# Sixteen experts in another order, a ring of 16 weight slots, and two projections 512 columns wide

## The chip, the cores and the metric

The kernel runs on one core of one Trainium2 chip. The time is device microseconds (us) from the start of the program to its end; the median of three runs is given, and one further execution was profiled. Five engines work from queues of their own: TensorE (PE; its weight loads are listed as PEld), VectorE (DVE), ScalarE (ACT), GpSimd (POOL) and SyncE (SP), which here does nothing but issue transfers from memory (DMA).

## The reference, cut to what matters

One transformer layer over 512 tokens of width 1024, all in float32: a mixer of three branches (forgetting attention, a pooling branch, a state-space branch called SSD), then a mixture of 16 experts.

```
proj = h @ w_in                       # q, k, v, z, xbc, gates, ... are columns of it
y_ssm = ssd_mixer(z, xbc, ...)        # y * silu(z) inside, then @ w_ssm_o
y_att = attention(q, k, v, log_f) @ w_attn_o
merged = g0 * y_att + g1 * y_pool + g2 * y_ssm
x = layer_norm(ALPHA * x + g_m * (merged @ w_out))
# each token goes to 2 of 16 experts, D = 1024, DFF = 512
expert(x, e) = (silu(x @ w1[e]) * (x @ w3[e])) @ w2[e]
x = layer_norm(ALPHA * x + g_f * (sum over its 2 experts of gate * expert(h, e)))
```

## The kernel before

**Stages.** In the profiled execution the normalisation and the modulation take the first 72 us, the state-space branch 72 to 505, pooling 505 to 614, attention 614 to 835, the output projection, the second normalisation and the routing up to about 990, the experts 990 to 1310, and the last sum and normalisation the rest.

**Three products for one.** `mm3` makes a float32 product out of three reduced-precision ones (hi by hi, hi by lo, lo by hi; lines 109 to 111). For that, every weight unit of 1 MB (128 partitions by 2048 numbers) is split in two halves: ACT casts it to the high part (line 90) and DVE, now and then POOL, subtracts that from it (line 91). `proj_n` makes a block of 128 tokens by 256 columns in one PSUM tile of which half is used: 24 matmuls of 256 columns. It serves the z projection (two units for each of four SSD groups) and the value projection (four units), 12 units by 4 blocks by 24 = 1152 matmuls in all.

**Experts in rounds.** `ROUNDS` is a list of 12 rounds. An entry is a position, not a fixed expert: `route` ranks the 12 dynamic experts by their number of tokens, and `RANK` gives the positions, the last one (15) to the largest. A round with one position is a full expert: up to 128 token rows, 6 weight units (four for gate and up, called A here, two for down, called D), 72 matmuls by `mm3`. A round with two is a pair of small experts with up to 64 rows each: 12 units, plain float32 in two column halves of the array (`pair_mm`, line 1364), no splitting. The largest expert gets two blocks of 128 rows; it stands behind the loop, in the end of `experts` and in `last`, and each of its six units is multiplied by both blocks. The loop runs A of round i, the transposes of the rows of round i+1, D of round i-1, the transposes of the activations. A round's result is scattered by token into `y_d` in memory (`put`, an indirect transfer from POOL). The two blocks of the largest expert aren't scattered: they stay on chip (`keep_y`), and matmuls with a one-hot matrix spread them over the tokens (`select`, `spread`, line 1435).

**Weights.** `self.src` is the order in which the 96 units are loaded, written out by hand: A of a round, then D of the round before. `take` hands out the next unit and issues the load of the one 16 places on, into a ring of 17 slots (`SLOTS`); the lower half of a split unit is written into the slot of the unit before it. All these loads stand in SP's queue (line 1201) and run in order; with `OUT = 2` a load is issued when the one two places before it has landed.

**The end.** `begin` (line 1405) loads `y_d` back, 1 MB for each of four token blocks, behind all weights in SP's queue. `gated` weighs the two results of a token and adds the residual: for blocks 0 and 2 two DVE instructions (lines 1419, 1420), for blocks 1 and 3 two scalings on ACT and two additions on POOL (lines 1416, 1417). `add` (line 1428) adds the spread part, and `end` normalises and stores.

Of the kernel before, what the change touches and what calls it, by code (L numbers as in the profile page):

```python
# [8 lines left out]
F32 = mybir.dt.float32  # L9
F32R = mybir.dt.float32r  # L10
# [31 lines left out]
         ("w", 0), ("w", 2), ("w", 4), ("w", 5), ("g", 0), ("x", 5), ("g", 2)]  # L42
Y = ("w", 2), ("w", 4), ("w", 5), ("g", 2)
# [3 lines left out]
ROUNDS = [(0,), (1,), (2,), (3,), (4, 5), (6,), (7,), (8, 9), (10,), (11, 12), (13,), (14,)]  # L47
NR = len(ROUNDS)
FULL = [e for r in ROUNDS if len(r) == 1 for e in r if e >= ST]
RANK = {E - 1: 0, **{e: i + 1 for i, e in enumerate(FULL)},  # L50
        **{e: i + 1 + len(FULL) for i, e in enumerate(e for r in ROUNDS if len(r) == 2 for e in r)}}
# [10 lines left out]
class Net:  # L62
# [375 lines left out]
    def ssd_proj(self, g):  # L438
# [29 lines left out]
        for u in range(2):  # L468
            wt = self.weights(self.I["wu"][5 * g + 3 + u])
            for b in range(NB):  # L470
                ps = self.proj_n(wt, b)
                t = T.tile([P, 256], F32, name="zt", tag="ztan", bufs=2)
                nc.scalar.activation(t, ps[:, :256], AF.Tanh, scale=0.5)
                nc.vector.scalar_tensor_tensor(zs[:, b, u * 256:(u + 1) * 256], t, 1.0, ps[:, :256],
                                               op0=OP.add, op1=OP.mult)
# [101 lines left out]
    def gate(self, br, u, bufs=2, tag="gt", pool=None):  # L577
        wt = self.weights(self.I["wu"][36 + br * 4 + u])
        out = []
        for j in range(2):  # L580
            ps = self.proj_t(wt, j)
            t = (pool or self.T).tile([P, S], F32, name="gt", tag=tag, bufs=bufs)
            self.nc.scalar.activation(t, ps, AF.Tanh, scale=0.5)
            out.append(t)
        return out

    def ssd_branch(self):
# [8 lines left out]
        for u in range(4):  # L596
            gts += self.gate(2, u, bufs=8, tag="gt2")
# [9 lines left out]
    def pool_branch(self):  # L607
# [8 lines left out]
        for g in range(4):  # L616
# [25 lines left out]
            gt = self.gate(1, g)  # L642
# [13 lines left out]
    def att_branch(self):  # L656
# [12 lines left out]
        with self.pool("attg") as self.T:  # L669
# [6 lines left out]
            for u in range(1, 4):  # L676
                gts += self.gate(0, u, bufs=6)
# [18 lines left out]
    def att_heads(self, out, O, gts):  # L696
# [4 lines left out]
        def values(u):  # L701
            wt = self.weights(self.I["wu"][20 + u])
            for b in range(NB):
                ps = self.proj_n(wt, b)
                nc.scalar.copy(vn[:, b, u * 256:(u + 1) * 256], ps[:, :256])

        for u in range(3):
            values(u)
            if not u:
                self.ada_end()  # L710
# [15 lines left out]
        values(3)  # L726
# [194 lines left out]
    def finish(self, X):  # L921
# [28 lines left out]
        down = lambda r: [(e, u) for u in (4, 5) for e in r]  # L950
        for i, r in enumerate(ROUNDS):
            src += [(e, u) for u in range(4) for e in r]
            if i:
                src += down(ROUNDS[i - 1])
        self.src = src + [(E - 1, 0)] + down(ROUNDS[-1]) + [(E - 1, u) for u in range(1, 6)]
        two = {e for r in ROUNDS if len(r) == 2 for e in r}
# [110 lines left out]
    def experts(self, X):  # L1067
# [11 lines left out]
        self.ix = self.K.tile([P, NR + 2, 2], I32, name="ix")  # L1079
# [6 lines left out]
        x = self.stage_x(X, self.xt[0])  # L1086
# [8 lines left out]
        pair = lambda i: i < NR and len(ROUNDS[i]) == 2  # L1095
        for i in range(NR):
            self.slots(X, i + 2)
            self.gather(i + 2)
            n = (self.pair_a if pair(i) else self.stage_a)(X, x, self.take)
            x = (self.pair_x if pair(i + 1) else self.stage_x)(X, self.xt[(i + 1) % 2])  # L1100
            if i:
                (self.pair_d if pair(i - 1) else self.stage_d)(X, a, self.ix[:, i - 1, 1:2], self.take)
            a = self.pair_t(X, *n) if pair(i) else self.stage_t(X, *n)
            if i == 4:
                self.weigh()
                more()
            if i == 4:
# [3 lines left out]
        keep = self.F2.tile([P, 2048], F32R, name="keep", tag="fraw0", bufs=1)  # L1111
        xs = [x, self.stage_x(X, self.xt[(NR + 1) % 2], self.spare())]
        pg = [self.mm_tile() for _ in range(2)]
        for u in range(2):
            w = self.take()
            for c in range(2):
                self.unit_a(pg[c], xs[c], w, u)
            if not u:
                self.stage_d(X, a, self.ix[:, NR - 1, 1:2], self.take)
                self.select(keep[:, D:])  # L1120
# [6 lines left out]
        return xs, pg, w, wd, keep  # L1127

    def last(self, X, xs, pg, w, wd, keep):
        nc, v = self.nc, self.nc.vector  # L1130
        pu = [self.mm_tile() for _ in range(2)]
        for c, u in ((0, 0), (1, 0), (0, 1)):
            self.unit_a(pu[c], xs[c], w[u], u)
        a = self.glu(pg[0], pu[0])
        self.unit_a(pu[1], xs[1], w[1], 1, (0, 1))
        t = [self.turn(X, a)]
        self.unit_a(pu[1], xs[1], w[1], 1, (2, 3))
        self.yx = [X.tile([P, 2, D], F32R, name="yx", tag="xraw5", bufs=1), self.F2.tile([P, 2, D], F32R, name="yx", tag="fraw1", bufs=1)]
        h = [slice(0, 512), slice(512, D)]

        def down(c, i):
            ps = self.mm_tile()
            ah, al = t[c]
            hi, lo = wd[i]
            for k in range(4):
                kc = slice(k * 512, (k + 1) * 512)
                self.mm3(ps, ah[:, k], al[:, k], hi[:, kc], lo[:, kc], k == 0, k == 3)
            return ps
# [4 lines left out]

        y = self.F.tile([P, D], F32, name="yb", tag="yb", bufs=1)
        ps = down(0, 0)
        a = self.glu(pg[1], pu[1])
        self.gated(0, 2)
        t.append(self.turn(X, a, keep))
        keep_y(0, 0, ps)
        self.gated(2, 4)  # L1160
        ps = down(0, 1)
        keep_y(0, 1, ps)
        ps = down(1, 0)
        keep_y(1, 0, ps)
# [12 lines left out]
    def select(self, room):  # L1177
        nc = self.nc
        self.sel = room[:, :].rearrange("p (c t) -> p c t", c=2)
        self.wy = self.K.tile([P, 2], F32, name="wy")  # L1180
        pw = self.aux_tile()
        for c, pos in enumerate((self.pp[:, :, ND - 1], self.pe)):
            g = self.K.tile([P, NB, P], F32, name="sel", tag="fr", bufs=1)
            pt = self.aux_tile()
            self.match(g, pos)
            for b in range(NB):
                self.transpose(pt[:, b * P:(b + 1) * P], g[:, b])
            for b in range(NB):
                nc.tensor.matmul(pw[:, c:c + 1], g[:, b], self.we1[:, b:b + 1], start=b == 0, stop=b == NB - 1)
# [16 lines left out]
    def take(self):  # L1206
# [9 lines left out]
        with ExitStack() as st:  # L1216
            if i in (1, 2, 3):
                st.enter_context(self.tc.issue_after(self.seen.ins))
                pool = (0, 1) if i == 3 else ()
# [3 lines left out]
            w = self.halves(raw, room, self.slot(i - (4 if self.whole[i - 1] else 1), F32R), pool)  # L1223
# [16 lines left out]
    def slots(self, X, r):  # L1240
# [3 lines left out]
        es = ROUNDS[r] if r < NR else (E - 1,)  # L1244
        pos = [self.pe if r > NR else self.p1[:, :, e] if e < ST else self.pp[:, :, e - ST] for e in es]
# [48 lines left out]
    def stage_a(self, X, x, take):  # L1294
        pg = []
        for m in range(2):
# [3 lines left out]
            pg.append(ps)  # L1300
        return pg

    def stage_t(self, X, g, u, room=None):
        return self.turn(X, self.glu(g, u), room)

    def glu(self, g, u):
        nc = self.nc
        a = self.K.tile([P, 512], F32, name="a", tag="fr", bufs=1)
        self.silu = nc.scalar.activation(a, g, AF.Silu)
        self.prod = nc.vector.tensor_tensor(a, a, u, OP.mult)  # L1310
        return a
# [55 lines left out]
    def pair_a(self, X, x, take):  # L1367
        pg = []
        for m in range(2):
# [3 lines left out]
            pg.append(ps)  # L1373
        return pg

    def pair_t(self, X, g, u):
        a = self.glu(g, u)
        pt = self.aux_tile()
# [21 lines left out]
    def begin(self, X):  # L1400
        nc = self.nc
        self.ys, self.zs = [], []
        for b in range(NB):
            y = self.slot(SLOTS.index(Y[b]))[:, :].rearrange("p (k d) -> p k d", k=2)
# [205 lines left out]
    def overflow(self, X):  # L1610
# [20 lines left out]
        rank, star = (K.tile([P, ND], F32, name=nm) for nm in ("rank", "star"))  # L1631
# [7 lines left out]
        v.tensor_copy(star, oh[:, ND - 1])  # L1639
# [12 lines left out]
        v.tensor_scalar(pe, pp[:, :, ND - 1], 128.0, None, op0=OP.subtract)  # L1652

        def more():
            n[0] = 0
            rooms[0] = K.tile([P, 512], F32, name="room", tag="fr", bufs=1)
            w1 = self.we1 = K.tile([P, NB], F32, name="we1")
            t, g1 = T(NB, ND), T(NB)
            for k in range(2):
# [155 lines left out]
```

## Time and profile before

| | us |
|---|---|
| median of three runs | 1335.49 (1333.13 to 1340.77) |
| profiled execution, its own time | 1343.89 |
| its span | 1341.9 |
| TensorE busy in the span | 1257.7 (94%) |
| VectorE, ScalarE, GpSimd busy | 920.7, 597.7, 241.4 |
| moved by DMA | 224.81 MB |

The profiled execution is 8.4 us, or 0.6%, above the median. In the views, `L109` is line 109 of the kernel; `mm<-whi,ht` names the destination and the operands by their names in the program; a row of waits reads "who waits <- for whom: total us, times, longest". The granted clock of TensorE is 1.00 at 2.4 GHz and 0.50 at 1.2 GHz; a stretch between them had both. Matmuls overlap: a start-to-start distance is the cost of one in a row of them, not its listed length.

### The profile page before, as it was taken

The page shows a single profiled execution, that of the slowest core. Times are in us where ns is not written, and L with a number is a line of the kernel's source. Part 1 is how long each engine was busy: PE and PEld are TensorE (multiplying, and loading weights), DVE is VectorE, ACT ScalarE, POOL GpSimd, SP SyncE. Part 2 cuts the span into 40 slices and gives each one's busy share as a digit, 9 for nine tenths or more (in the row PEclk, how much of TensorE's full clock was granted, in tenths as well). Part 3 has the DMA queues.
Part 4 walks back from the last instruction along what each step waited for, and adds up shares of the span by engine and source line. Part 5 has one row for each costly group of instructions (what it writes and reads, how often), then busy time and mean ns, then how long its engine had stood idle before and what let it go on. Part 6 is the DMA issues. An engine that isn't in the chain of part 4 may idle for free. (4 is left out here: it accounts for less than half of the span.)

```text
span 1341.9 us, 17467 instructions
## 1 busy us (share of the span) xinstructions
PE 1257.7 (94%) x6561; PEld 992.2 (74%) x6561; DVE 920.7 (69%) x1498; ACT 597.7 (45%) x1084; POOL 241.4 (18%) x186
## 2 busy tenths in 40 slices
PE   6999999999999999999999999999859999888992
PEld 3788887887887888889977777888647756535781
DVE  6796856667667348794288888486878786515776
ACT  2456463462462324333357667331236554414642
POOL 3501010010010000000111210132233423203253
PEclk6799999999999999999999999999878998999996
DMA  8421111211211228755211103228567989999941
GB/s 337 157 95 64 63 64 63 95 63 63 95 64 63 94 95 320 262 201 193 94 60 63 63 32 124 96 94 331 204 224 284 332 307 334 345 339 336 328 192 64
DMA packets 37766, 224.81 MB, mean 168 GB/s; under 512 B 5411, under 2 KB 5955, under 8 KB 13488
## 3 DMA queue, kind: packets, MB, share of 16 engines
q1 hardware_dynamic: 31008, 208.54, 43.1%
q0 software_dynamic: 4032, 8.84, 1.8%
q10 hardware_dynamic: 2640, 6.29, 1.3%
q8 instruction: 53, 0.87, 0.3%
q14 instruction: 33, 0.27, 0.1%
HBM read 214.80 MB, written 14.70 MB: 171 GB/s over the span
## 5 line engine op out<-in xcount | busy, mean ns | idle before, releaser
L91 DVE TENSOR_TENSOR raw<-raw,whi 128x1024 fp32r<-128x1024 f32 x234 | 291.9, 1264 | 153.4 <-ACT whi L90 133.0
L90 ACT CAST whi<-raw 128x1024 fp32r<-128x1024 f32 x248 | 252.5, 1053 | 149.5 <-PE mm L110 105.6
L109 PE MATMUL mm<-ht,whi 128*128 128x512 f32 x576 | 232.2, 403 | 0.0
L110 PE MATMUL mm<-ht,whi 128*128 128x512 f32 x576 | 228.8, 397 | 0.0
L111 PE MATMUL mm<-ht,raw 128*128 128x512 f32 x576 | 228.5, 397 | 0.0
L109 PE MATMUL mm<-whi,ht 128*128 128x256 f32 (+1 forms) x448 | 135.9, 304 | 0.6 <-DVE cacc L434 0.4
L111 PE MATMUL mm<-whi,ht 128*128 128x256 f32 (+1 forms) x448 | 135.5, 303 | 0.0
L110 PE MATMUL mm<-raw,ht 128*128 128x256 f32 (+1 forms) x448 | 135.4, 302 | 0.0
L111 PEld LDWEIGHTS mm<-ht,raw 128*128 128x128 f32 x576 | 109.3, 190 | 22.2 <-issue 0.2
L109 PEld LDWEIGHTS mm<-ht,whi 128*128 128x128 f32 x576 | 109.7, 191 | 21.0 <-issue 0.9
L110 PEld LDWEIGHTS mm<-ht,whi 128*128 128x128 f32 x576 | 109.5, 190 | 21.0 <-issue 0.7
L109 PEld LDWEIGHTS mm<-whi,ht 128*128 128x128 f32 x448 | 86.1, 192 | 5.8 <-issue 2.7
L111 PEld LDWEIGHTS mm<-whi,ht 128*128 128x128 f32 x448 | 86.3, 193 | 5.0 <-issue 2.4
L110 PEld LDWEIGHTS mm<-raw,ht 128*128 128x128 f32 x448 | 86.2, 193 | 4.5 <-issue 1.8
L110 PE MATMUL mm<-raw,xh 128*128 128x512 f32 x160 | 67.6, 422 | 11.7 <-DVE raw L91 8.0
L109 PE MATMUL mm<-whi,xh 128*128 128x512 f32 x160 | 66.7, 417 | 2.8 <-ACT whi L90 1.7
L111 PE MATMUL mm<-whi,xl 128*128 128x512 f32 x160 | 65.1, 409 | 0.0
L521 POOL TENSOR_TENSOR y<-xsn,small 128x512 f32<-128x512 f32 x16 | 19.8, 1246 | 227.1 <-ACT xsn L452 139.0
L434 DVE SCALAR_TENSOR_TENSOR cacc<-mm,small,cacc 128x511 f32<-128x511 f32 (+2 forms) x72 | 52.9, 743 | 9.3 <-ACT cacc L432 8.7
L110 PE MATMUL mm<-yl,whi 128*128 128x512 f32 x128 | 53.0, 414 | 0.0
L109 PE MATMUL mm<-yh,whi 128*128 128x512 f32 x128 | 52.1, 407 | 0.0
L111 PE MATMUL mm<-yh,raw 128*128 128x512 f32 x128 | 50.8, 397 | 0.0
(427 smaller groups left out, 2422.9 us busy)
## 6 DMA issues: line engine op xcount, KB each, us to landing
raw<-in_we_dram SPq DMA_DIRECT2D x96, 1024.0 KB, 6.7
raw<-in_wu_dram SPq DMA_DIRECT2D x48, 1024.0 KB, 5.0
ra<-in_wada_dram SPq DMA_DIRECT2D x24, 1024.0 KB, 6.9
raw<-in_wso_dram SPq DMA_DIRECT2D x8, 1024.0 KB, 5.1
x<-in_x_dram SPq DMA_DIRECT2D x8, 512.0 KB, 8.2
y_d<-zero ACTq DMA_DIRECT2D x1, 4096.0 KB, 18.1
raw<-in_wao_dram SPq DMA_DIRECT2D x4, 1024.0 KB, 4.9
raw<-in_wout_dram SPq DMA_DIRECT2D x4, 1024.0 KB, 4.8
```

The costliest lines, as they stand in the source:

```text
L90: h = self.nc.scalar.copy(hi, src)
L91: self.cut = [h, (eng or self.nc.vector).tensor_tensor(lo, src, hi.bitcast(F32), OP.subtract)]
L109: mm(ps, lh, rh, start=first, stop=False)
L110: mm(ps, lh, rl, start=False, stop=False)
L111: self.last_mm = mm(ps, ll, rh, start=False, stop=last)
L434: nc.vector.scalar_tensor_tensor(acc[:, i:], ps[:, :S - i], w(3 - i), acc[:, i:], op0=OP.mult, op1=OP.add)
L521: nc.gpsimd.tensor_tensor(h8(y[:, :]), h8(xsn[:, b]), b8(s[:, S_DSK + g * 8:S_DSK + g * 8 + 8]), OP.mult)
```

## The change

**Rounds.** There are 13: positions 0, 1, 2, 3, the pair (4, 5), 6, the pair (7, 8), the two-block expert (9, 9), then 10, 11, 12, 13, and the pair (14, 15) last. The work is the same: nine full experts, three pairs, one expert with two blocks, 96 units. The two-block expert is a round of the loop (`star_a`, `star_d`), its two results are scattered like the others, and it uses all four PSUM tiles of the name `mm` at a time. Now the last two rounds, expert 13 and the pair, stay on chip and are spread.

**Ring.** 16 slots rather than 17; the room set free is the second block's in the two-block round, later that of a `y_d` block.

**`y_d`.** Three of its four blocks are loaded ahead of the last four weight units in SP's queue, the fourth behind them. The first block needs the last scatter, now that of round 10; the second and third go into slots that the pair's first units leave.

**Projections.** `proj_n` makes 512 columns at once: two units of half the depth, four PSUM tiles open through both, 576 matmuls of 512 columns. The tanh of z and the copy of v take 512 columns too.

**Smaller edits.** The silu of an expert stands directly behind its gate product. Unit 3 is split by DVE alone, no longer by POOL. `more` works out weights for three experts rather than one, about ten small DVE instructions more. `gate` of the branches is renamed.

```diff
 SLOTS = [("f", 0), ("f", 1), ("w", 3), ("w", 1), ("g", 1), ("x", 4), ("x", 0), ("x", 1), ("x", 2), ("x", 3),
-         ("w", 0), ("w", 2), ("w", 4), ("w", 5), ("g", 0), ("x", 5), ("g", 2)]
-Y = ("w", 2), ("w", 4), ("w", 5), ("g", 2)
+         ("w", 0), ("w", 2), ("w", 4), ("w", 5), ("g", 0), ("g", 2)]
-ROUNDS = [(0,), (1,), (2,), (3,), (4, 5), (6,), (7,), (8, 9), (10,), (11, 12), (13,), (14,)]
+ROUNDS = [(0,), (1,), (2,), (3,), (4, 5), (6,), (7, 8), (9, 9), (10,), (11,), (12,), (13,), (14, 15)]
...
-    def proj_n(self, wt, b):
-        hi, lo = wt
-        ps = self.mm_tile()
-        for k in range(KD):
-            c = slice(k * 256, (k + 1) * 256)
-            t = slice(b * P, (b + 1) * P)
-            h, l = self.hs(k)
-            self.mm3(ps[:, :256], h[:, t], l[:, t], hi[:, c], lo[:, c], k == 0, k == KD - 1)
-        return ps
+    def proj_n(self, u, then):
+        ps = [self.mm_tile() for _ in range(NB)]
+        for i in range(2):
+            hi, lo = self.weights(self.I["wu"][u + i])
+            for b in range(NB):
+                t = slice(b * P, (b + 1) * P)
+                for j in range(4):
+                    c = slice(j * 512, (j + 1) * 512)
+                    h, l = self.hs(i * 4 + j)
+                    self.mm3(ps[b], h[:, t], l[:, t], hi[:, c], lo[:, c], i == j == 0, i == 1 and j == 3)
+                if i:
+                    then(b, ps[b])
...
-        self.src = src + [(E - 1, 0)] + down(ROUNDS[-1]) + [(E - 1, u) for u in range(1, 6)]
+        self.src = src + of(NR - 1, (0,)) + of(NR - 2, (4, 5)) + of(NR - 1, range(1, 6))
...
+        self.select(X)
+        pg = self.mm_tile()
+        self.pair_mm(pg, x, 0, [self.take(), self.take()], True, False)
         w = [self.take() for _ in range(2)]
-        wd = [self.take() for _ in range(2)]
-        self.begin(X)
-        self.rows = self.F.tile([P, 2048], F32, name="rows", tag="graw0", bufs=1)
+        raws = [self.take() for _ in range(6)]
+        self.begin(X, range(3))
+        raws += [self.take() for _ in range(4)]
+        self.begin(X, (3,))
...
-                pool = (0, 1) if i == 3 else ()
+                pool = ()
...
+    def star_a(self, X, xs, take):
+        ps = [[self.mm_tile() for _ in range(2)] for _ in range(2)]
+        for m in range(2):
+            for u in range(2):
+                w = take()
+                for c in range(2):
+                    self.unit_a(ps[c][m], xs[c], w, u)
+        out = []
+        for c in range(2):
+            out.append(self.gate_up(self.gate(ps[c][0], X.tile([P, 512], F32, name="a2", tag="al2", bufs=1) if c else None), ps[c][1]))
+        return out
...
+        for i in range(2):
+            ps = self.mm_tile()
+            for k in range(4):
+                kc = slice(k * 512, (k + 1) * 512)
+                self.mm3(ps, act[0][:, k], act[1][:, k], w[i][0][:, kc], w[i][1][:, kc], k == 0, k == 3)
+            keep_y(0, i, ps)
+        self.pair_mm(pg, x, 4, raws[0:2], False, True)
+        a = self.gate(pg)
+        pu = self.mm_tile()
+        self.pair_mm(pu, x, 0, raws[2:4], True, False)
+        self.pair_mm(pu, x, 4, raws[4:6], False, True)
+        a = self.gate_up(a, pu)
         pz = self.sums()
         self.spread(pz, 0, 0)
-        ps = down(1, 1)
+        at = self.pair_t(X, a, self.mm_tile())
+        ps = self.mm_tile()
+        self.pair_mm(ps, at, 0, raws[6:8], True, True)
+        self.gated(0, 2)
+        keep_y(1, 0, ps)
+        self.gated(2, 3)
+        ps = self.mm_tile()
+        self.pair_mm(ps, at, 0, raws[8:10], True, True)
         self.spread(pz, 1, 0)
         keep_y(1, 1, ps)
+        self.gated(3, 4)
```

**Where instructions stand now.** First TensorE in the first SSD group, at the end of the z projection (`ht` are the transposed activations, `whi` and `raw` the high and low parts of a weight unit; the rows on `xdt`, `st` and `xde` are the SSD chunks that stand between). Before:

```order
L109 MATMUL mm<-whi,ht_88 128x256
L110 MATMUL mm<-raw,ht_88 128x256
L111 MATMUL mm<-whi,ht_88 128x256
L519 MATMUL aux<-xdt,sc 128x64 x2
L524 MATMUL aux<-st,cmt 128x512
L529 MATMUL aux<-xde,bmn 128x512
L109 MATMUL mm<-ht_85,whi 128x512
L110 MATMUL mm<-ht_85,whi 128x512
L111 MATMUL mm<-ht_85,raw 128x512
```

And with the change:

```order
L112 MATMUL mm<-whi,ht_88 128x512
L113 MATMUL mm<-raw,ht_88 128x512
L114 MATMUL mm<-whi,ht_88 128x512
L524 MATMUL aux<-xdt,sc 128x64 x8
L534 MATMUL aux<-xde,bmn 128x512
L524 MATMUL aux<-xdt,sc 128x64 x8
L112 MATMUL mm<-ht_85,whi 128x512
L113 MATMUL mm<-ht_85,whi 128x512
L529 MATMUL aux<-st,cmt 128x512
L534 MATMUL aux<-xde,bmn 128x512
```

Each matmul of the projection writes 512 columns rather than 256 and there are half as many; the next product (`mm<-ht_85,whi`) follows in both.

Second, SyncE's queue at the end of the experts (each load of a unit, `raw<-in_we_dram`, has a register instruction ISA ahead of it that picks the expert). Before:

```order
L1201 DMA raw<-in_we_dram 128x2048
L1201 ISA
L1201 DMA raw<-in_we_dram 128x2048
L1028 TENSOR_LOAD nob
L1028 ISA x2
L1405 DMA raw<-y_d 128x2048 x4
L1126 DMA rows<-in_rows_dram 128x1024 x2
```

And with the change:

```order
L1217 DMA raw<-in_we_dram 128x2048
L1457 DMA raw<-y_d 128x2048 x3
L1217 ISA
L1217 DMA raw<-in_we_dram 128x2048
L1217 ISA
L1217 DMA raw<-in_we_dram 128x2048
L1217 ISA
L1217 DMA raw<-in_we_dram 128x2048
L1217 ISA
L1217 DMA raw<-in_we_dram 128x2048
L1457 DMA raw<-y_d 128x2048
L1146 DMA raw<-in_rows_dram 128x1024 x2
```

Three of the four loads of `y_d` have moved ahead of the last four weight units, and all that stands behind them waits for them to be issued.

Third, TensorE at its end (`whi,keep` and `yx,keep` belong to the two-block expert before; `raw,xh` and `raw,ah` are the pair's products after, L1487 the spreading). Before:

```order
L109 MATMUL mm<-whi,keep 128x512
L110 MATMUL mm<-raw,keep 128x512
L111 MATMUL mm<-whi,keep 128x512
L1435 MATMUL aux<-yx,keep 128x512 x8
L1435 MATMUL mm<-yx,keep 128x512 x16
```

And with the change:

```order
L113 MATMUL mm<-raw,ah_10207 128x512
L114 MATMUL mm<-whi,al_10208 128x512
L1415 MATMUL mm<-raw,xh 64x512 x24
L1487 MATMUL aux<-raw 128x512 x8
L156 MATMUL mm<-consts,a 128x128 x4
L1415 MATMUL mm<-raw,ah_10392 64x512 x16
L1487 MATMUL aux<-raw 128x512 x8
L1487 MATMUL mm<-raw 128x512 x16
```

The three-product matmuls of the largest expert are gone from the end; what stands there is the pair's gate and up products (24), its down products (16 in two calls) and the same number of spreading matmuls (32).

## Rows read from the trace of the kernel before

**Rows 1.** The page: span, TensorE's share, granted clock in 40 slices.
```profile
span 1341.9 us, 17467 instructions
...
PE 1257.7 (94%) x6561; PEld 992.2 (74%) x6561; DVE 920.7 (69%) x1498; ACT 597.7 (45%) x1084; POOL 241.4 (18%) x186
...
PEclk6799999999999999999999999999878998999996
```

**Rows 2.** Windows by stage: length; busy PE, PEld, DVE, ACT, POOL; clock; DMA share; GB/s.
```profile
72.00:505.00 433.00, 428.71 (x2380) 357.52 (x2379) 283.41 (x413) 194.16 (x391) 29.57 (x27) 1.00 0.22 74
...
1277.50:1310.00 32.50, 32.07 (x149) 25.87 (x147) 24.76 (x20) 14.54 (x18) 16.18 (x7) 1.00 0.42 171
1310.00:1342.00 32.00, 7.62 (x24) 5.59 (x24) 21.41 (x40) 8.32 (x13) 8.86 (x8) 0.66 0.17 67
```

**Rows 3.** Windows as in rows 2, inside the expert stage, by rounds.
```profile
1015.00:1067.00 52.00, 51.92 (x271) 42.14 (x269) 47.17 (x44) 37.67 (x47) 21.24 (x13) 1.00 0.90 323
1067.00:1125.00 58.00, 53.24 (x263) 32.49 (x260) 42.79 (x93) 28.42 (x36) 18.52 (x11) 0.94 0.89 319
1125.00:1186.00 61.00, 57.22 (x280) 32.50 (x280) 28.97 (x32) 22.63 (x29) 15.78 (x10) 1.00 0.94 343
1186.00:1242.00 56.00, 48.07 (x215) 23.91 (x211) 22.45 (x26) 18.65 (x25) 12.17 (x8) 0.97 0.94 333
1242.00:1277.00 35.00, 33.13 (x142) 25.64 (x143) 26.21 (x27) 24.74 (x31) 10.44 (x7) 0.95 0.92 334
```

**Rows 4.** Timeline of TensorE in a z projection: start, length, operation.
```profile
273.77 0.28 PE L109 MATMUL mm<-whi,ht 128*128 128x256 f32 x1
...
279.76 0.28 PE L111 MATMUL mm<-whi,ht 128*128 128x256 f32 x1
```

**Rows 5.** Timeline of TensorE in the output projection, 512 columns.
```profile
917.15 0.39 PE L109 MATMUL mm<-whi,ht 128*128 128x512 f32 x1
...
922.19 0.40 PE L110 MATMUL mm<-raw,ht 128*128 128x512 f32 x1
```

**Rows 6.** Waits of SyncE's queue, 1040 to 1300: total, times, longest.
```profile
SPq L1201 <- DMA raw<-in_we_dram: 187.9, 65, 5.5
SPq L1405 <- DMA y_d<-yb,ix: 10.7, 1, 10.7
...
SPq L1201 <- PE mm L111: 0.4, 1, 0.4
```

**Rows 7.** Timeline of SyncE's queue, 990 to 1300.
```profile
997.41 275.70 SPq L1201 DMA_DIRECT2D raw<-in_we_dram  x80
1284.47 1.97 SPq L1405 DMA_DIRECT2D raw<-y_d  x4
```

**Rows 8.** Busy time in 4 us stretches around the last loads.
```profile
1278.00:1282.00 4.00, 4.00 (x24) 3.45 (x23) 3.98 (x4) 2.88 (x5) 3.37 (x3) 1.00 0.00 0
...
1290.00:1294.00 4.00, 4.00 (x18) 3.00 (x16) 2.94 (x3) 1.98 (x2) 0.00 (x0) 1.00 1.01 428
```

**Rows 9.** Gate and up products of one pair (line 1364 alone).
```profile
1067.00:1081.00 14.00, 13.95 (x64) 4.51 (x64) 1.00 0.92 329
```

**Rows 10.** Timeline of TensorE at the end.
```profile
1309.18 0.39 PE L111 MATMUL mm<-whi,keep 128*128 128x512 f32 x1
...
1313.67 3.36 PE L1435 MATMUL aux<-yx,keep 128*128 128x512 f32 x7 [0.23 <-DVE yx L91]
1316.82 3.97 PE L1435 MATMUL mm<-yx,keep 128*128 128x512 f32 x16
```

**Rows 11.** Timeline of VectorE at the end.
```profile
1319.45 0.69 DVE L1428 SCALAR_TENSOR_TENSOR z<-mm,z 128x512 f32<-128x512 f32 x1 [1.36 <-PE mm L1435]
```

**Rows 12.** Groups of instructions from 1305 to the end: busy, mean ns.
```profile
L1417 POOL TENSOR_TENSOR z<-raw,z 128x1024 f32<-128x1024 f32 x1 | 3.2, 3223 | 0.1
...
L1416 ACT ACTIVATE raw<-raw,gw 128x1024 f32<-128x1024 f32 x1 | 1.1, 1137 | 0.0
```

**Rows 13.** Timeline of VectorE early in the expert stage.
```profile
1000.28 1.23 DVE L91 TENSOR_TENSOR raw<-raw,whi 128x1024 fp32r<-128x1024 f32 x1 [4.67 <-POOL raw L91]
```

More of the change, by code (lines that the diff above doesn't have):

```diff
@@ L467, in ssd_proj, with gated @@
         zs = T.tile([P, NB, 512], F32, name="zs", tag="zs", bufs=1)
[L468 to L475, printed above, removed]
+        def gated(b, ps):
+            t = T.tile([P, 512], F32, name="zt", tag="ztan", bufs=1)
+            nc.scalar.activation(t, ps, AF.Tanh, scale=0.5)
+            nc.vector.scalar_tensor_tensor(zs[:, b], t, 1.0, ps, op0=OP.add, op1=OP.mult)
+        self.proj_n(5 * g + 3, gated)
         return xsn, sc, cmt, bmn, zs
@@ L701, in values @@
         def values(u):
[L702 to L710, printed above, removed]
+            self.proj_n(20 + 2 * u, lambda b, ps: nc.scalar.copy(vn[:, b, u * 512:(u + 1) * 512], ps))
+        values(0)
+        self.ada_end()
         half = [slice(0, 64), slice(64, P)]
@@ L1094, in experts @@
         a = None
[L1095 to L1100, printed above, removed]
-            if i:
-                (self.pair_d if pair(i - 1) else self.stage_d)(X, a, self.ix[:, i - 1, 1:2], self.take)
-            a = self.pair_t(X, *n) if pair(i) else self.stage_t(X, *n)
+        for i in range(NR - 1):
+            for j in lines[i]:
+                if j + 2 < len(LINES):
+                    self.slots(X, j + 2)
+                    self.gather(j + 2)
+            k = KIND[i]
+            n = self.star_a(X, x, self.take) if k == "S" else (self.pair_a(X, x, self.take) if k == "P" else
+                                                               self.stage_a(X, x[0], self.take))
+            x = rows(i + 1)
+            if i:
+                down(i - 1, a)
+            if k == "S":
+                a = [self.turn(X, n[1], self.room[:, D:])]
+                a.insert(0, self.turn(X, n[0]))
+            else:
+                n = self.gate_up(*n)
+                a = self.pair_t(X, n) if k == "P" else self.turn(X, n)
             if i == 4:
@@ L1110, in experts @@
                         nc.scalar.mul(x1[:, b], x1[:, b], ALPHA)
[L1111 to L1120, printed above, removed]
@@ L1125, in experts, with last @@
+        self.rows = self.slot(6)
         for i in range(2):
             nc.sync.dma_start(self.rows[:, i * D:(i + 1) * D], self.I["rows"][2 + i:3 + i, :].to_broadcast([P, D]))
-        return xs, pg, w, wd, keep
-    def last(self, X, xs, pg, w, wd, keep):
+        return x, a, pg, w, raws
+    def last(self, X, x, act, pg, w, raws):
         nc, v = self.nc, self.nc.vector
[L1131 to L1138, printed above, removed]
-        h = [slice(0, 512), slice(512, D)]
[L1141 to L1148, printed above, removed]
+        self.yx = [self.slot(k, F32R)[:, :].rearrange("p (k d) -> p k d", k=2) for k in (5, 4)]
+        h = [slice(0, 512), slice(512, D)]
+        y = self.F.tile([P, D], F32, name="yb", tag="yb", bufs=1)
@@ L1222, in take @@
                     st.enter_context(self.tc.issue_after(m.ins))
[L1223 removed]
+            w = self.halves(raw, room, self.slot(i - (4 if i and self.whole[i - 1] else 1), F32R), pool)
         self.halved = self.cut
@@ L1773, in _layout @@
         us.append(unit((x0 + 2048 + i * P, P), (x0 + 2560 + i * P, P)))
-        us += [unit((z0 + i * 512 + j * 256, 256)) for j in range(2)]
-    us += [unit((v0 + i * 256, 256)) for i in range(4)]
+        us += wide(z0 + i * 512)
+    us += wide(v0) + wide(v0 + 512)
     us += [unit((q0 + i * P, P), (k0 + i * P, P)) for i in range(8)]
```

165 lines of the change are left out of this document (100 added, 65 removed).

## The prediction

> **What bounds the kernel now.** I began with the page: TensorE is busy for 94% of the span, so what it doesn't have to do, or does without waiting, is what time can come from; the clock slices fall to 6 or 7 tenths around slice 30 and in the last slice [rows 1]. The windows by stage show two kinds of stage. From 72 to 505 TensorE is busy 428.71 of 433 us at full clock while the DMA engines are at 0.22: nothing but TensorE bounds the state-space stage [rows 2]. The experts differ. Between 1015 and 1277 the DMA share stands at 0.89 to 0.94, and TensorE's busy time falls short of the windows by 0.08, 4.76, 3.78, 7.93 and 1.87 us, 18.4 in all; its clock of 0.94, 0.97 and 0.95 in three of them is another (0.06 x 58) + (0.03 x 56) + (0.05 x 35) = 6.9 us of lost work [rows 3]. So there the two are nearly in balance, transfers a little ahead. That transfers pace the loads, not the ring, is in SyncE's waits: 65 waits of 187.9 us for an earlier load to land, 0.4 us for a slot that a matmul holds [rows 6]. The queue issues 80 loads in 275.70 us, 3.49 us each [rows 7], and a TensorE pitch of 0.229 us (below) makes 72 matmuls of a full expert 16.5 us plus transposes, against 6 x 3.49 = 20.9 us for its units: transfers are the slower. A pair's gate and up products take 13.95 us as 64 records [rows 9], so its 96 records take about 21 us, against 12 x 3.49 = 41.9 us of transfers. Only the two-block expert is the other way round: 144 matmuls are 33 us, with transposes and `select` some 36, against 20.9.
>
> And this one expert stands last. After the last weight has landed, nothing is transferred from 1278 to 1282 [rows 8], and from 1277.5 to 1310 TensorE works 32.07 of 32.5 us with transfers at 0.42, most of that being `y_d` [rows 2]. The last down matmul is at 1309.18, the spreads end near 1320.8, `add` on the second half starts at 1319.45, and the span ends 22.45 us later [rows 10, 11].
>
> **The projections.** In the old z projection 50 steps take 279.76 - 273.77 = 5.99 us, 120 ns for 256 columns [rows 4]. The new form has a neighbour in the trace: the output projection with the same operand kinds at 512 columns takes 922.19 - 917.15 = 5.04 us for 22 steps, 229 ns [rows 5]. So 576 pairs of narrow matmuls become wide ones at 576 x (0.240 - 0.229) = 6.3 us less, all on the engine that bounds those stages. What stood behind them is the same; the tiles wait for one tanh of 512 columns where they waited for two of 256, and four tiles stay open over two units, so the first matmul of the next product may wait for VectorE to empty one. I take 0.8 us off for that: -5.5 us, with -3 to -7.5 as bounds.
>
> A rule speaks against that term: the Trainium skill, "TensorE: Matmul & The Clock Gate", section "Back-to-back issue gap", gives an isolated gap of N/2.4 + 2.5 ns, so that a wide matmul would save 2.5 ns against two narrow ones, 576 x 2.5 ns = 1.4 us in all by that page, and the sum would be 4 us less. This trace disagrees about the narrow one: it measures 120 ns at 256 columns where the rule gives 109, and the measurement decides.
>
> **The last weight.** The order of rounds doesn't change the 96 units, so the stream ends where it did, 1277.5, plus what now stands in front of its end. Three `y_d` blocks of 1 MB: at the 428 GB/s that the re-read reached 2.45 us each [rows 8], at the 343 GB/s of the weights 3.06 [rows 3], so 7.4 to 9.2, taken as 8.5. One slot less in the ring: at most one unit, 3.5 us; since slots hold nobody up [rows 6], I take 2. The stream must not stop during the two-block round: TensorE takes 36 us there, transfers could bring 36 / 3.49 = 10 units, and the round itself has six, so the lead grows by four or five, in a ring of 15 ahead. The last unit lands at about 1288 (1285 to 1291).
>
> **TensorE behind it.** Behind the last unit stand 8 matmuls, 16 records of 0.218 us: 3.5 us, so 1291.5 at the earliest. TensorE's own bound: its end of 1309.5, less the 18.4 us it waited and 6.9 of low clock, is 1284 if all came back. It won't: the pairs keep their waits, and each round has short ones for VectorE. With half of the 25 given back it ends at 1297. The two bounds are so close that I take 1295 for the last down matmul. From there to the first `add` of the second half 9.9 us passed before (1309.57 to 1319.45), with 23 spreads in 7.1 us at half or mixed clock [rows 10]. The same chain stands there now: 1305. At full clock the spreads give back some 2 us; both ends are in the range. Beside it, the fourth `y_d` block lands about 3 us behind the last weight, then needs one scaling of 1.14 us and two POOL additions of 3.22 us [rows 12] before its first `add`: 1291 + 7.6 = 1299, hidden. The rest is what it was, 22.45 us. So this part gives 1305 - 1319.45 = -14.5 us, with -8 (TensorE ends at 1301) and -20 (ends at 1291.5, spreads at full clock) as bounds.
>
> **The small edits.** Unit 3 on POOL made VectorE wait 4.67 us [rows 13]; two halves of about 1.23 us on VectorE itself take 2.5, so some 2 us come earlier, while the ring is still full and the transfer end doesn't feel it. The ten extra instructions of `more`, at 0.15 to 0.3 us by the small rows around there an estimate of 2 us, lie on VectorE in a pair's round, whose products need no splitting. The two-block round drains four tiles at once and loses perhaps 1 us. Silu earlier gives that back. Together 0, from -3 to +3.
>
> **Sum.** 1343.89 - 14.5 - 5.5 = 1323.9 us for the profiled execution. It lies 0.6% above the median; in the median's terms 1335.49 x 1323.9 / 1343.89 = **1315.6, say 1315 us**. The likeliest case alone, both terms within their bounds: 1308 to 1324.
>
> **Rivals.**
> 1. *The stream stands still in the two-block round*, because the slots are full or a load waits behind one that can't be issued. The round then costs its 36 - 21 = 15 us of idle transfers; the last unit lands at 1303, the last matmul is at 1306.5, `add` near 1316.5. Gain 3 + 5.5: 1327. Against it: 15 slots by 3.49 us are 52 us of cover.
> 2. *Slower: the `y_d` loads block the queue.* The first waits for round 10's scatter; before, the load at 1284.47 had waited 10.7 us for its scatter [rows 6, 7], with nothing behind it but the vectors `rows`. Now the last four units stand behind it, 14 us of transfers. SyncE comes to it ten units behind round 10's down units; the scatter needs about 10.7 us, three units. So waiting begins if the stream is seven units ahead of TensorE, and each unit beyond that costs 3.49 us one for one. To undo 20 us and be slower by 0.5% (6.7 us) it takes 27 us, eight units: the stream as far ahead as the ring allows. That gives about 1343.
> 3. *The clock.* It stood at 0.66 in the last window [rows 2], and was low near 1112 and 1201 where pairs made TensorE pause (0.94, 0.97 in those windows) [rows 3]. A pair that waits for transfers is now last: its 32 down records and 32 spreads at 1.2 GHz cost 7 + 3 us more at worst; half is nearer to what a pair in the loop shows. 1321 to 1325.
> 4. *Width saves nothing*: 512 columns cost twice the 120 ns of 256 in these stages, or the four open tiles give the saving back. The term is 0: 1321. For it: four tiles are all there are. Against it: the 229 ns [rows 5]. The page named above is nearest to this case.
> 5. *More comes back*: TensorE waits almost nowhere before the last pair, and the state-space stage loses its short waits as well (433 - 428.71 = 4.3 us [rows 2]). Both terms at their better bound are 7.5 us more, half of the 4.3 another 2: 1305, down to 1303.
>
> **Chances.** Likeliest 0.47; rival 1 0.12; rival 2 0.06; rival 3 0.13; rival 4 0.08; rival 5 0.14. 0.5% is 6.7 us, about what a measurement of this kernel can tell from no change. Faster by more (below 1328.8): the likeliest, 3, 4, 5 in full, and half of 1, less some mishap that I don't see: 0.82. Within: 0.12. Slower: rival 2, 0.06. A range of 1301 to 1331 takes in the likeliest, 3, 4, most of 5 and of 1.
>
> **What would show it.** In the changed profile: 512-column matmuls of the z projection at about 229 ns start to start, and the state-space stage 3 to 5 us shorter; the last unit landing near 1288 less that saving, with no gap in transfers in the two-block round; `y_d` loads of which the first is issued without a long wait; the last down matmul 3.5 us behind the last unit or a little later; `add` on the second half about 22.5 us ahead of the end. I am wrong if SyncE waits for a slot or for a scatter by more than 10 us, if TensorE still idles 18 us between 1015 and 1277, or if the end behind the last unit is longer than 40 us.

## The result, and the profile after

The changed kernel takes 1325.12 us (median of 7 runs, 1318.89 to 1331.53) against 1336.96 us (7 runs of the kernel before in the same comparison): a ratio of 0.9917, 95% interval 0.9895 to 0.9938. That is 11.8 us less by the medians, where 20 were forecast; faster, at little more than half the size. It lies inside the range, 1 us outside the likeliest case (1308 to 1324). The profiled execution took 1328.39 us, 15.5 us less than the profiled one of before.

The page of the changed kernel, as in [rows 1]:

```profile
span 1326.6 us, 16285 instructions
...
PE 1243.0 (94%) x5992; PEld 960.5 (72%) x5993; DVE 916.6 (69%) x1501; ACT 594.8 (45%) x1058; POOL 234.3 (18%) x182
...
PEclk6799999999999999999999999999968998898996
```

TensorE has the same 94%; its busy time is down by 14.7 us. The timeline of TensorE in the z projection, the wide form against [rows 4]:

```profile
269.99 0.40 PE L114 MATMUL mm<-whi,ht 128*128 128x512 f32 x1
...
275.92 0.39 PE L113 MATMUL mm<-raw,ht 128*128 128x512 f32 x1
```

26 steps in 5.93 us are 228 ns. The first product of an expert starts 6.3 us earlier than before (982.34 against 988.67), 1 us of which is there before the first projection.

From that first product to the last down product it was 320.9 us before and is now 311.9. From the last down product to the end it was 32.3 us and is 32.4. The timeline of SyncE's queue from 940 on and its waits from 980 on, against [rows 6, 7], which begin at 1040 and 990:

```profile
941.52 305.93 SPq L1217 DMA_DIRECT2D raw<-in_we_dram  x84
1265.70 2.40 SPq L1457 DMA_DIRECT2D raw<-y_d  x3
1268.35 14.72 SPq L1217 DMA_DIRECT2D raw<-in_we_dram  x4
1283.17 0.37 SPq L1457 DMA_DIRECT2D raw<-y_d  x1
```

```profile
SPq L1217 <- DMA raw<-in_we_dram: 207.8, 72, 10.8
...
SPq L1457 <- DMA y_d<-yb,ix: 18.2, 1, 18.2
```

Nothing went to the queue between the load that began before 1247.45 and 1265.70: it stood 18.2 us at the first `y_d` load for round 10's scatter. The windows of the expert stage, columns as in [rows 2]; the two-block expert is TensorE's work from about 1142 to 1197, with the second pair's down products and the next expert's gate and up products between its own:

```profile
1084.00:1120.00 36.00, 30.00 (x131) 15.25 (x131) 23.03 (x87) 4.94 (x7) 6.46 (x6) 0.91 0.92 343
1120.00:1138.00 18.00, 16.23 (x71) 7.82 (x68) 7.30 (x10) 5.71 (x8) 1.89 (x1) 0.83 0.91 336
1138.00:1176.00 38.00, 36.69 (x183) 26.43 (x183) 18.04 (x20) 18.10 (x23) 12.72 (x7) 0.99 0.94 353
1176.00:1200.00 24.00, 24.00 (x119) 19.61 (x118) 19.37 (x23) 13.94 (x16) 8.30 (x5) 1.00 0.91 310
1200.00:1225.00 25.00, 20.06 (x99) 15.98 (x98) 16.98 (x18) 14.54 (x18) 5.75 (x3) 0.86 0.92 354
1225.00:1245.00 20.00, 20.00 (x95) 16.49 (x94) 17.55 (x15) 15.99 (x20) 9.38 (x6) 1.00 0.87 326
1245.00:1273.00 28.00, 27.34 (x140) 19.56 (x139) 19.95 (x21) 13.43 (x18) 7.23 (x6) 1.00 0.50 179
1273.00:1300.00 27.00, 26.33 (x119) 11.91 (x117) 12.35 (x18) 7.22 (x9) 6.17 (x3) 1.00 0.69 271
```

Between 1084 and 1138, around the second pair, TensorE stands for 7.8 us, and the granted clock of the two windows is 0.91 and 0.83. From 1200 to 1225 it stands for 4.9 us, at a clock of 0.86. From 1225 on it has next to no gap, while transfers fall to 0.50 in the window in which SyncE stands: TensorE doesn't wait for transfers there. Its wait at the second of these places, and the timeline of VectorE:

```profile
PE mm L113 <- DVE raw L94: 4.9, 1, 4.9
```

```profile
1206.83 1.29 DVE L1348 TENSOR_TENSOR yb<-mm,gf 128x512 f32<-128x512 f32 x2 [7.09 <-DMA y_d<-yb,ix]
...
1208.64 8.57 DVE L94 TENSOR_TENSOR raw<-raw,whi 128x1024 fp32r<-128x1024 f32 x7
```

Line 1348 multiplies the second block's result into `yb`. That buffer exists once, and the first block's scatter still reads it: VectorE waits 7.09 us, and behind it in its queue stand the activations' low half and seven weight halves (8.57 us). One of these halves is what TensorE waits 4.9 us for.

The ends, TensorE first, then VectorE, against [rows 10, 11]:

```profile
1273.44 10.52 PE L1415 MATMUL mm<-raw,xh 128*64 128x512 f32 x48
...
1287.15 7.09 PE L1415 MATMUL mm<-raw,ah 128*64 128x512 f32 x32 [0.67 <-ACT ah L1432]
1294.16 2.12 PE L1487 MATMUL aux<-raw 128*128 128x512 f32 x8
1296.12 3.95 PE L1487 MATMUL mm<-raw 128*128 128x512 f32 x16
```

```profile
1294.81 1.28 DVE L1472 SCALAR_TENSOR_TENSOR z<-raw,gw,z 128x1024 f32<-128x1024 f32 x1
1296.02 0.75 DVE L1156 SCALAR_TENSOR_TENSOR yb<-mm,wy,gf 128x512 f32<-128x512 f32 x1
...
1303.38 0.69 DVE L1480 SCALAR_TENSOR_TENSOR z<-aux,z 128x512 f32<-128x512 f32 x1 [3.41 <-POOL z L1469]
...
1304.00 0.69 DVE L1480 SCALAR_TENSOR_TENSOR z<-mm,z 128x512 f32<-128x512 f32 x1
```

TensorE is through at 1300.07, 20.7 us earlier than before: 5.9 us behind its last down product instead of 11.2, with the spreads at full clock and without the wait that stood there before:

```profile
1312.94 0.50 PE L1435 MATMUL aux<-yx,keep 128*128 128x512 f32 x1 [3.37 <-ACT yx L90]
```

But the weighing of block 2 (line 1472) stands ahead of the last result (line 1156), and the last block's first `add` waits 3.41 us for POOL. So `add` on the second half starts at 1304.00, 9.8 us behind the last down product, as before.

### The profile page after: what moved, and what is told of

Same layout as the page of the kernel before. It is cut to its first block, busy times and chain, and to the rows that moved or that the text cites. A ratio compares the mean times of both kernels' runs of the same rounds, so it can differ in the third digit from the quotient of the medians.

```text
span 1326.6 us, 16285 instructions
## 1 busy us (share of the span) xinstructions
PE 1243.0 (94%) x5992; PEld 960.5 (72%) x5993; DVE 916.6 (69%) x1501; ACT 594.8 (45%) x1058; POOL 234.3 (18%) x182
## 5 line engine op out<-in xcount | busy, mean ns | idle before, releaser
L112 PEld LDWEIGHTS mm<-ht,whi 128*128 128x128 f32 x576 | 110.0, 191 | 23.1 <-ACT whi L93 2.1
L113 PEld LDWEIGHTS mm<-ht,whi 128*128 128x128 f32 x576 | 110.0, 191 | 20.7 <-issue 0.5
L114 PE MATMUL mm<-whi,ht 128*128 128x512 f32 x256 | 101.4, 396 | 0.0
L112 PE MATMUL mm<-whi,ht 128*128 128x512 f32 x256 | 101.0, 396 | 0.3 <-DVE cacc L440 0.3
L113 PE MATMUL mm<-raw,ht 128*128 128x512 f32 x256 | 101.1, 395 | 0.0
L113 PEld LDWEIGHTS mm<-raw,ht 128*128 128x128 f32 x256 | 48.1, 188 | 12.2 <-issue 2.6
L114 PEld LDWEIGHTS mm<-whi,ht 128*128 128x128 f32 x256 | 48.0, 188 | 12.1 <-issue 2.6
L112 PEld LDWEIGHTS mm<-whi,ht 128*128 128x128 f32 x256 | 48.1, 188 | 11.7 <-issue 2.2
```

What stands on the lines that cost most here:

```text
L112: mm(ps, lh, rh, start=first, stop=False)
L113: mm(ps, lh, rl, start=False, stop=False)
L114: self.last_mm = mm(ps, ll, rh, start=False, stop=last)
```

## The experiments

Each was timed in five rounds against the kernel before on the same chip, in three batches on three chips: the first four runs below, the next four and the last four. So medians compare within a batch, and ratios across them. Theory A at the start: a wait in the two-block round and the order of work at the end hold the time, and TensorE bounds the stage behind that round. The rival is the prediction's own picture, that the last weight's landing sets the end.

**The changed kernel again** (`after_again`), the measure for the next three.

> The changed kernel once more, beside the experiments on the same chip, so that they are compared with it and not only with the kernel before. Expected: a ratio to the kernel before of 0.992 as measured first (0.9895 to 0.9938), some 1325 us.

Measured: 1326.28 us, ratio 0.9917 (0.9892 to 0.9943). The same.

**A result buffer of its own for the second block** (`yb2`).

```diff
-            y = self.F.tile([P, D], F32, name="yb", tag="yb", bufs=1)
+            y = X.tile([P, 2048], F32, name="yb2", tag="xraw5", bufs=1)[:, :D] if c else self.F.tile([P, D], F32, name="yb", tag="yb", bufs=1)
```

> The second block of the two-block expert gets a result buffer of its own (the room that its activations leave), so VectorE no longer waits for the first block's scatter. In the changed kernel VectorE stood 7.09 us there, TensorE 4.9 us for a weight half behind it, and the clock of 1200 to 1225 was 0.86. Theory A (TensorE bounds the rounds after the two-block expert, so the wait was lost for good): that wait is gone and the end comes 5 to 8 us earlier than in the changed kernel, about 1318 us. Rival (the loads set the end, as the prediction had it): TensorE gets there sooner and waits for weights later, 0 to 1 us.

Measured: 1319.69 us, ratio 0.9855 (0.9830 to 0.9881), 6.6 us less than the changed kernel by medians. The same line of VectorE and the same window:

```profile
1199.81 1.29 DVE L1348 TENSOR_TENSOR yb<-mm,gf 128x512 f32<-128x512 f32 x2 [2.11 <-PE mm L114]
...
1201.09 1.22 DVE L94 TENSOR_TENSOR raw<-raw,whi 128x1024 fp32r<-128x1024 f32 x1
```

```profile
1200.00:1225.00 25.00, 25.00 (x137) 20.41 (x136) 22.18 (x25) 19.21 (x23) 10.61 (x7) 1.00 0.92 322
```

The wait is gone, the window is full and its clock 1.00. Theory A holds: one buffer too few cost more than the projections gave.

**The weighing ahead of the last results** (`both`), on top of `yb2`.

```diff
-        self.gated(0, 2)
+        self.gated(0, 3)
         keep_y(1, 0, ps)
-        self.gated(2, 3)
+        self.gated(3, 4)
...
         keep_y(1, 1, ps)
-        self.gated(3, 4)
```

> As yb2, and the weighing of token blocks 2 and 3 is written ahead of the last split of the results instead of behind it. In the changed kernel the first add of the last part waited 3.41 us for POOL, whose scaling on ScalarE stood behind the last cast, and VectorE weighed block 2 for 2.5 us ahead of the last result. Theory A: 3 to 5 us less than yb2, about 1314 us. Rival (the fourth block lands too late, so that ScalarE waits for it and the cast behind it too): 0, or 1 to 2 us more.

Measured: 1316.41 us, ratio 0.9835 (0.9809 to 0.9861); 3.3 us less than `yb2` by medians, though the intervals of the two overlap. VectorE's timeline at the last adds:

```profile
1293.19 0.69 DVE L1479 SCALAR_TENSOR_TENSOR z<-aux,z 128x512 f32<-128x512 f32 x1 [0.47 <-POOL z L1468]
...
1293.80 0.69 DVE L1479 SCALAR_TENSOR_TENSOR z<-mm,z 128x512 f32<-128x512 f32 x1
```

The wait for POOL is 0.47 us instead of 3.42 in `yb2`, and the second half's first `add` starts 6.1 us behind the last down product (1287.7) instead of 9.8 there.

**4 MB more around the two-block round** (`extra4`).

```diff
-        self.loads.append(self.nc.sync.dma_start(raw, src))
+        for _ in range(2 if i in (48, 52, 56, 60) else 1):
+            self.loads.append(self.nc.sync.dma_start(raw, src))
```

> Units 48, 52, 56 and 60, around the two-block expert, are loaded twice into their slot: 4 MB more through the same queue, 4 x 3.49 = 14 us of transfers, nothing else. Theory A (TensorE bounds the end, transfers stood idle for 13 us from 1253 to 1266 waiting for a scatter): 0 to 4 us more than the changed kernel, and that idle stretch shrinks. Rival (the last weight sets the end): 10 to 14 us more.

Measured: 1336.69 us, ratio 0.9984 (0.9967 to 1.0001), 10.4 us more than the changed kernel. Theory A is wrong here, or I placed the loads wrongly. The waits of TensorE:

```profile
PE mm L113 <- DVE raw L94: 7.6, 6, 3.4
PE aux L156 <- DMA xt<-h_d,ix: 6.8, 1, 6.8
...
PE mm L112 <- ACT whi L93: 3.3, 2, 1.7
```

The gather of token rows (`xt`) took 6.8 us of TensorE's time, against 3.2 in two waits before the edit, and units 48 and 52 belong to the down products of position 6 and the up products of the two-block expert, next to the place where the changed kernel stands already (1084 to 1138). SyncE's wait for the scatter, which was to shrink, stayed (18.6 us). So I split the theory: transfers have no slack up to the two-block round; behind it they do (theory B).

**The same 4 MB behind it** (`extra4b`): units 68, 72, 76 and 80 in the line above.

> As extra4, but the four loads that are doubled are units 68, 72, 76 and 80, all behind the two-block expert. In extra4 the loss of 10 us lay ahead of it and inside it: TensorE waited 6.8 us for a gather of rows and 3.4 and 3.3 for split weights, and ran on at low clock. Theory B (transfers bound up to the two-block expert, TensorE behind it, where SyncE stands 18 us waiting for a scatter): 0 to 3 us more than the changed kernel, and the wait for the scatter shrinks by about 14 us. Rival (the last weight sets the end): 10 to 14 us more.

Measured: 1332.53 us, ratio 0.9957 (0.9935 to 0.9978): 5.3 us more than 0.9917, between the two expectations and wide. SyncE's wait:

```profile
SPq L1458 <- DMA y_d<-yb,ix: 15.6, 1, 15.6
```

It shrank by 2.6 us, not by 14. At 3.3 us a load (48 in 159.5 us of its queue) the four extra ones pass from about 1165 to 1215, an estimate; TensorE's waits that come with them, mostly for split weights, lie between 1220 and 1260 (6.0 us, 0.7 in the changed kernel). So some 9 of the 14 us were slack, less than I had said: neither TensorE nor the transfers bound this stage alone.

**The projections alone** (`proj_only`): the new `proj_n`, its two callers and the layout of their weights in the kernel before; the diff of `proj_n` is shown above.

> The kernel before with the 512-column projections alone; rounds, ring and end as before. My term was -5.5 us (-3 to -7.5), and the changed kernel's trace reaches its first expert product 6.4 us earlier than before, 1 us of that from the start of the span. Expected by the 229 ns pitch: 5 to 6 us less, a ratio of 0.996. Rival (width saves nothing): 0 to 1.5 us, 0.999 to 1.000. A third way, that the experts' transfers take the saving back, would show a trace with that lead at the first expert product and none at the end.

Measured: 1332.56 us, ratio 0.9959 (0.9943 to 0.9976): 5.5 us, the predicted term. Its queue, against [rows 7], and TensorE's waits in its expert stage:

```profile
940.51 306.05 SPq L1197 DMA_DIRECT2D raw<-in_we_dram  x88
1272.20 2.04 SPq L1401 DMA_DIRECT2D raw<-y_d  x4
```

```profile
PE mm L110 <- DVE raw L91: 9.8, 12, 3.5
PE aux L153 <- DVE a L1306: 4.7, 3, 3.0
PE mm L110 <- POOL raw L91: 3.8, 3, 1.7
```

By chance this execution also tests the prediction's main step. With the order of before, the last weight was issued at 1246.6, against 1273.1 in the profiled execution of before: 26.5 us earlier, of which 7.3 are there at the first product of an expert. The last down product came at 1297.3 instead of 1309.6, and from the first product it was 316.0 us instead of 320.9. Within the stage the last weight moved by some 19 us and the end by 5.

In `yb2`, the new order without VectorE's wait for the scatter, that stage takes 308.2 us, and TensorE's waits from 1000 on are these:

```profile
PE aux L156 <- DMA xt<-h_d,ix: 5.2, 2, 3.2
PE aux L156 <- DVE a L1361: 4.0, 2, 3.1
PE mm L113 <- DVE raw L94: 2.9, 3, 1.2
```

Over the whole stage the waits for split weights (`raw` on VectorE and POOL) are 4.5 us, against 13.6 with the old order. Waits for the gather (`xt`, 5.2 us) are new. In all TensorE stands for 15.8 us in the stage, against 22.0 in `proj_only`. That is what the order gives, together with the ring and the smaller edits; no run takes the order by itself.

**All `y_d` loads behind the weights** (`both_ylast`), on top of `both`.

```diff
-        self.begin(X, range(3))
         raws += [self.take() for _ in range(4)]
-        self.begin(X, (3,))
+        self.begin(X)
```

> The kernel both, with all four loads of the scattered results behind the last weights in the queue, so that no weight waits for a scatter. Theory B (TensorE bounds the end; the weights behind the scatter come early enough as it is): within 2 us of both. Rival (the blocked queue makes the last pair's weights late): 3 to 8 us less than both. A second rival: the fourth block lands later behind the others and the last adds wait for it: 1 to 4 us more.

Measured: 1317.10 us, ratio 0.9841 (0.9813 to 0.9870), against 0.9835: the same. Its queue:

```profile
940.02 317.98 SPq L1215 DMA_DIRECT2D raw<-in_we_dram  x88
1262.04 2.02 SPq L1455 DMA_DIRECT2D raw<-y_d  x4
```

And in `both`, with its wait for the scatter:

```profile
1261.84 14.20 SPq L1216 DMA_DIRECT2D raw<-in_we_dram  x4
```

```profile
SPq L1456 <- DMA y_d<-yb,ix: 8.8, 1, 8.8
```

The last weight is now issued at 1258.0 rather than at 1276.0, and the time stays. A queue blocked for 8.8 us cost nothing that can be told, nor did the late fourth block; the 18.2 us of the changed kernel were not tested this way.

**Unit 3 split by POOL again** (`pool3`).

```diff
-                pool = ()
+                pool = (0, 1) if i == 3 else ()
```

> The changed kernel with unit 3 split by POOL again. I had put this edit at 0 (-3 to +3): VectorE stood 4.67 us for POOL's half early in the expert stage, but the ring was full there. If TensorE bounds the end of the stage while the pairs in the middle wait for transfers, a late start is taken back in the middle: 0 to 1 us more than the changed kernel. Rival (each us at the start stays to the end): 2 to 3 us more.

Measured: 1328.23 us, ratio 0.9918 (0.9897 to 0.9940), against 0.9917: no difference, as the prediction had put it.

**The place of the two-block expert.** `both` again, and two orders of its rounds:

```diff
-ROUNDS = [(0,), (1,), (2,), (3,), (4, 5), (6,), (7, 8), (9, 9), (10,), (11,), (12,), (13,), (14, 15)]
+ROUNDS = [(0,), (1,), (2,), (3,), (4, 5), (6,), (7, 7), (8, 9), (10,), (11,), (12,), (13,), (14, 15)]   # star_first
+ROUNDS = [(0,), (1,), (2,), (3,), (4, 5), (6,), (7, 8), (9,), (10,), (11, 11), (12,), (13,), (14, 15)]  # star_late
```

> The kernel both once more, as the measure for the two orders below on the same chip: 0.9835 of the kernel before (0.9809 to 0.9861), some 1316 us.

> The kernel both with the two-block expert one round earlier, ahead of the second pair: rounds ..., (6,), (7, 7), (8, 9), (10,), .... What is left of TensorE's waiting lies around the second pair (1084 to 1138: 8 us idle and a clock of 0.91 and 0.83), before the two-block expert has put the loads ahead. Theory B (there transfers and gathers are late, TensorE bounds the rest): the pair finds its units landed, 2 to 5 us less than both. Rival (those waits are for VectorE and for the gather of the two blocks' rows, whatever stands ahead): 0, within 2 us.

> The kernel both with the two-block expert two rounds later, behind two more full experts: rounds ..., (7, 8), (9,), (10,), (11, 11), (12,), (13,), (14, 15). A full expert takes TensorE about 18.7 us and 6 units of transfers 20.9, so by theory B the lead of the loads shrinks further ahead of it, and TensorE waits: 2 to 5 us more than both. Rival (TensorE bounds these rounds too, the place makes no difference): within 2 us.

Measured: `both` 1315.24 us, 0.9824 (0.9800 to 0.9848); `star_first` 1315.42 us, 0.9817 (0.9794 to 0.9841), the same; `star_late` 1321.97 us, 0.9881 (0.9857 to 0.9905), 6.7 us more. TensorE's waits in `star_late`:

```profile
PE mm L113 <- DVE raw L94: 6.2, 9, 1.6
...
PE mm L113 <- POOL raw L94: 3.2, 3, 1.7
```

In `both` the first of these is 4.5 us over the same stretch and the second is missing. (This profiled execution was the fastest of its five, 1316.82 us, so the 6.7 us can't be read off it.) Two full experts more between the second pair and the two-block one cost time; one round earlier doesn't change it: there the waits for the gather (4.2 us) and for the silu product (4.0) all but vanish and those for split weights rise from 4.5 to 13.0.

**One slot less in the kernel before** (`ring16`): `("x", 5)` taken out of `SLOTS`.

> The kernel before with a ring of 16 slots instead of 17, nothing else. My term for the slot was 2 us (0 to 3.5) on the landing of the last weight. By SyncE's waits (0.4 us for slots) and with TensorE as the bound: 0, a ratio of 0.999 to 1.001. Rival (each load starts one unit later): 2 to 3.5 us more, 1.002 to 1.003.

Measured: 1348.26 us, ratio 1.0078 (1.0054 to 1.0102), more than the rival said. But the edit did more than I meant. SyncE's waits at the `y_d` loads:

```profile
SPq L1405 <- PE mm L111: 16.4, 2, 10.4
...
SPq L1405 <- DVE raw L91: 11.6, 1, 11.6
SPq L1405 <- PE mm L110: 8.3, 1, 8.3
```

With 16 slots the four that `y_d` is loaded into hold units 91, 92, 93 and 95, still in use at the end; before, the loads waited only for a scatter [rows 6]. From the first to the last down product that execution, the fastest of its six, took 318.2 us, between 316.0 and 320.9; behind it the end took 39.1 us instead of 32.3. So the loss that this trace shows lies in the late `y_d`, and the slot's own price isn't told by this run. The changed kernel moved `y_d` to slots that are free earlier; this shows what not doing so costs.

## Why the prediction came out as it did

**The projections** were right in mechanism and size: 5.5 us forecast, 5.5 measured with the edit alone, at 228 ns where 229 were assumed. The gap rule of the Trainium skill, "TensorE: Matmul & The Clock Gate", section "Back-to-back issue gap", which the page gives for isolated matmuls, would have made it an estimated 1.4 us; the measured time, -3.2 to -7.6 us by the interval, disagrees with it.

**The order of rounds** was forecast at -14.5 us. The change gives 0.9917 where the projections alone give 0.9959: some 5.6 us. The step that was mis-sized is "The two-block round drains four tiles at once and loses perhaps 1 us". The tiles weren't what it waited for. The round scatters two blocks through one buffer `yb`, VectorE waited 7.09 us for the first scatter, and `yb2` measured the price, 6.6 us by medians, 8.3 by the ratios. Without it the ratio is 0.9855, 13.9 us below `proj_only` (8.9 between the two profiled executions). In the profiled execution of `yb2`, the slowest of its five, the last down product ends at 1289.5, the 1295 of the text less its 5.5. That it fits to the tenth is luck: the 1295 was chosen between two bounds, and the next paragraph takes one of them away. In the changed kernel TensorE still stood 15.9 us between 1010 and 1273 (1.2 of it ahead of the windows shown), against 18.4 before [rows 3]; 18 was one of the signs that the text had named for being wrong. The kernels' text shows the single buffer (`bufs=1`), and the trace of before shows a scatter's 10.7 us wait [rows 6]; I had priced that wait at the queue and not at the buffer.

**The last weight** was the wrong reason. The text let its landing near 1288 set the end, with TensorE's own bound close beside it. The waits of SyncE [rows 6] say only that each load is issued behind an earlier one, which holds whenever two are allowed under way and a slot is free. In `proj_only` the stream ended far earlier and the stage hardly shortened; in `both_ylast` the same. What the stage of `yb2` has less of is TensorE's waiting for split weights, 13.6 to 4.5 us. I had read these gaps as late transfers. `extra4`, `extra4b` and `star_late` show that transfers still matter: 14 us more of them cost 10 and 5 us. How much of each wait is the loads and how much the splitting stays open.

**The end** had the right sum for two wrong reasons. It took 9.9 us from the last down product to `add`, measured 9.8. But TensorE was through 5.3 us sooner behind its last down product: its 3.6 us of waiting for the split result are gone, and the full clock gave 1.7 (24 spreads in 5.9 us instead of 7.6), near the 2 of the text. All of it went to the weighing in the wrong place; `both` got some 3 back. The fourth block was put down as hidden at 1299; it lands in time, but its scaling on ScalarE stood in the queue behind a cast at 1296.80.

**The base.** The forecast started from a profiled execution of 1343.89 us, 5 to 8 us above the medians of before (1335.5 to 1339.3). Its expert stage took 4.9 us more than that of `proj_only` in the same order (TensorE busy 297.8 against 294.0 us, idle 23.1 against 22.0), so some of what I handed back wasn't typical. Part of it was also counted twice: from 1110 to 1114 the clock of 0.78 means 1.8 us at the lower level, and TensorE worked only 1.1 us there, so some of the 6.9 us of low clock lies in its idle time.

**The rivals.** 1, a stream that stands still in the two-block round: no, the share is 0.91 to 0.94 there. 2, the blocked queue: its trigger came about, 18.2 us, one of the signs that I named for being wrong; the price "one for one" did not follow, since TensorE still had work: between 1260 and 1300 its only wait in the trace is the 0.67 us for `ah`, and none for a weight. In `yb2` that load waited 6.9 us. 3, the clock: 1.00 from 1273 to 1300. 4, width without a gain: no. 5, more comes back: no; `both` and `star_first`, at 0.982 to 0.984, come near the central 1315 and not to its 1305.

## What to carry to other kernels

When work that was kept on chip is sent through an existing path, count the buffers of that path: two results in a row through one buffer make the second wait for the first transfer, and an engine that works its queue in order, as VectorE did here, holds back everything behind it. A queue that mostly waits for its own transfers isn't proof that transfers set the end; look at an execution in which they happen to run faster, or add some and see what each costs. In a tail, write what can be ready early (the weighing of what has landed) ahead of what arrives last.

## What the runs showed that I had not expected

The transfers of weights ran at different rates in executions of the same stretch: the last unit was issued 26.5 us earlier in `proj_only` than in the profiled execution of before, and TensorE's last down product came only 12.3 us earlier. Delaying the re-read of `y_d` in the kernel before, as `ring16` did, cost 0.8%, while 8.8 us of standing queue in `both` cost nothing that can be told.
